# Products of two heads given to TensorE in turn, on different rows or columns of its array

## The chip, the core and the metric

The kernel runs on one core of a Trainium2 chip, as one launch. The metric is the device time of that launch in microseconds (us): the median of three runs of the kernel before is 3310.76 us (3308.05 to 3312.59). The profiled execution is a run of its own; its trace lists each instruction with its engine, its line in the kernel and the names of the tiles it writes and reads. PE is TensorE, DVE VectorE, ACT ScalarE, POOL GpSimd.

## The reference

Two layers act on 512 latent tokens and 256 context tokens of width 1024. Each layer is: half-step SwiGLU feed-forward, token mixing, half-step SwiGLU feed-forward, each with RMS norm and a shift, scale and gate from a conditioning vector. Token mixing projects the tokens with one matrix and gives the columns to four groups of heads that work side by side. Their outputs are concatenated and projected back.

- GLA: 4 heads with keys of 32 and values of 64, gated linear attention in chunks of 64 tokens, both directions in time.
- Mamba-2 (SSD): 4 heads of 64 in 2 groups with a state of 64, chunks of 64, both directions.
- RWKV-7: 4 heads of 64, a recurrence whose state is changed by a rank-one term at each token, both directions.
- Attention: 4 query heads and 2 key heads of 64, softmax over latents and context.

The second layer needs no context output. The products in question are the small ones inside the chunks, for instance in GLA

```
q_dec = q * jnp.exp(b)
att = jnp.einsum('bnthd,bnshd->bnhts', q_dec, k * jnp.exp(-b))
att = jnp.where(causal, att, 0.0)
```

and in SSD `cb = einsum('bctgn,bcsgn->bcgts', cc, bc)`. For RWKV-7 the kernel does not step token by token: it writes a chunk as products of 64x64 matrices, with the inverse of a triangular matrix for the rank-one terms.

## The kernel before, in words

Activations lie transposed, features on the 128 partitions and tokens along the free dimension. So a head of 64 features occupies 64 partitions and two heads (a pair, index `hp`, and `e` or `hh` within it) fill one tile. A product of one head has its contraction on 64 (GLA: 32) of the array's 128 rows, or its output on 64 of the 128 columns. All of these products are float32, and the program's float32 product appears in the trace as two MATMUL records (called passes here), each with its own weight load.

`mix` (L1783 on) runs one layer's token mixing in two stages. The first stage opens pools with two PSUM banks for the tag `pg` (GLA), two for `ps` (SSD and RWKV preparation) and two double banks for the projections (`proj`, tile `pj`). In program order it holds:

- `rwkv_inverses`, which calls `x_rwkv_n` for each direction, pair and block of 256 tokens: per head four 64x64 products, a masking on DVE (L1330) and two DMAs to a DRAM tile `nd`. From `nd`, `x_rwkv_inverse` (L1398 on) later inverts the triangular matrices on DVE, 31 steps of two instructions (L1410, L1412) per direction.
- `x_gla_in`, `x_gla_dir`, `x_ssm_in`, then `x_gla_block` (L931) per block: per head four products into one bank `pg`, a masking on DVE (L944) into `am`, an addition on POOL into `a2`.
- `x_ssm`: per block and group two products (tile `cb`, L1077 to L1086), each group masked on DVE.
- The two inversions, the gates, the attention's inputs and the last projections.

The second stage (`open_second`, then `rwkv`) has three PSUM banks `pr` for RWKV, two `pc` for its recurrent steps, two `sc` and one `po`. The order of RWKV's pieces is written out by hand in `SCHEDULE`: U prepares a unit (one direction, one block; `x_rwkv_unit`), S solves it (`x_rwkv_solve`), T makes one recurrent step per chunk of 64 (`x_rwkv_step`), Y forms the outputs of a block (`x_rwkv_y`). There are six units per layer. The output projection of the other groups (`x_out`, tiles `yp`, `woh`, `wol`) and the attention (`x_att`) are written behind it.

The program's order is only the input of the framework's planner: the planner simulates the engines with its own costs and lays a fixed order for each engine. Each engine then takes its instructions in that order; PE's queue has products of projections, `x_out` and attention laid between RWKV's.

The places that the change touches:

- `x_rwkv_n`: head after head; both heads write partitions 64 to 127 of a bank of their own, and each is masked alone with 64 partitions.
- `x_rwkv_unit`: per pair, head `e` after head `e` (contraction on rows `es`), each in its own bank `pr`, each followed by one or two maskings (L1377). Then transposes (L1381), then eight products per pair into partitions 64 to 127 of one bank per pair, copied by ACT to the lower half of `ZV`; then transposes of `Bh` (L1394).
- `x_rwkv_solve`: after the solve, the product `pw` runs with its two heads in turn on different columns (`pw[64 * e:64 * e + 64, ...]`); the last eight products per pair go to partitions 64 to 127 of one bank per pair, copied back to `ZV`.
- `x_rwkv_y`: for every chunk and pair one product of 128 rows and columns with the state `H`, then two products of 128 rows and 64 columns (`ZV` with `A1`).

Of the kernel before, what the change touches and what calls it, by code (L numbers as in the profile page):

```python
# [7 lines left out]
F32 = mybir.dt.float32  # L8
# [4 lines left out]
ALU = mybir.AluOpType  # L13
# [5 lines left out]
D = 1024  # L19
# [33 lines left out]
class Net:  # L53
# [877 lines left out]
    def x_gla_block(self, l, b, D, yg):  # L931
        nc, gw = self.nc, self.gw
        mask = self.c("mgb", 256).rearrange("p (d t) -> p d t", d=2).unsqueeze(1).to_broadcast([128, 2, 2, 128])
        am = []
        for hh in range(4):
            hs = slice(32 * hh, 32 * hh + 32)
            pa = self.bank("pg")
            for tt in range(2):
                t = 2 * b + tt
                ts = slice(128 * t, 128 * t + 128)  # L940
                for d in range(2):
                    self.mm(pa[:, 256 * tt + 128 * d:256 * tt + 128 * d + 128], D[d][1][hs, ts], D[d][0][hs, ts])
            w = gw.tile([128, 2, 2, 128], F32, tag="am", name="am")
            nc.vector.tensor_tensor(w, pa.rearrange("p (t d x) -> p t d x", t=2, d=2), mask, op=ALU.mult)  # L944
            a2 = gw.tile([128, 2, 128], F32, tag=f"a2{hh}", name="a2", bufs=1)
            nc.gpsimd.tensor_tensor(a2, w[:, :, 0], w[:, :, 1], op=ALU.add)
            am.append(a2)
# [115 lines left out]
    def x_ssm(self, l, F, dts, need_ctx):  # L1063
        nc, gw = self.nc, self.gw
        nt = NT if need_ctx else NX
        blocks = (2, 0, 1) if need_ctx else (0, 1)
        x0, x1, Bf, Cf = F
# [7 lines left out]
        cb = [self.gt(f"cb{g}", (6, 128)) for g in range(2)]  # L1075
        both = self.c("bones", 128)
        for b in blocks:  # L1077
            for g in range(2):
                gs = slice(64 * g, 64 * g + 64)
                pb = self.bank("ps")  # L1080
                for tt in range(2):
                    t = 2 * b + tt
                    ts = slice(128 * t, 128 * t + 128)
                    self.mm(pb[:, 128 * tt:128 * tt + 128], Bf[gs, ts], Cf[gs, ts])
# [6 lines left out]
        for g in range(2):  # L1091
# [48 lines left out]
        for d in range(2):  # L1140
# [20 lines left out]
            for r in range(2):  # L1161
# [3 lines left out]
                pss = [self.bank("ps"), self.bank("ps")]  # L1165
                for n in order:
                    t, e = divmod(n, 2)
                    es = slice(64 * e, 64 * e + 64)
                    for g in range(2):
                        self.mm(pss[e][64 * g:64 * g + 64, 64 * t:64 * t + 64], BT[es, t, 64 * g:64 * g + 64], xw[r][es, t, g])  # L1170
                for n, nx in zip(order, order[1:]):
                    t, e = divmod(n, 2)
                    nc.vector.scalar_tensor_tensor(out=Sr[:, nx], in0=Sr[:, n], scalar=dec[r][:, n:n + 1],
                                                   in1=pss[e][:, 64 * t:64 * t + 64], op0=ALU.mult, op1=ALU.add)
            for b in blocks:
                bs = slice(256 * b, 256 * b + 256)
# [136 lines left out]
    def x_rwkv_n(self, hp, d, b, U, dec, nd):  # L1313

        nc, gw = self.nc, self.gw
        kk, bb = U
        P, iP = dec
        cs = slice(4 * b, 4 * b + 4)
        w = lambda z: z[:, 256 * b:256 * b + 256].rearrange("p (c t) -> p c t", t=64)
        mask = self.c("mr", 256)[64:128, 128 * d:128 * d + 64].unsqueeze(1).to_broadcast([64, 4, 64])  # L1320
# [3 lines left out]
        A = self.gx.tile([128, 2, 4, 64], F32, bufs=2, tag="wb", name="ns")  # L1324
        for hh in range(2):
            hs = slice(64 * hh, 64 * hh + 64)
            pss = self.bank()
            for c in range(4):
                self.mm(pss[64:128, 64 * c:64 * c + 64], R[hs, c, 0], R[hs, c, 1])
            nc.vector.tensor_tensor(A[64:128, hh], pss[64:128, 0:256].rearrange("p (c t) -> p c t", c=4), mask, op=ALU.mult)  # L1330
            for i in range(2):
                self.load(nd[i, hp, hh, cs].rearrange("c s t -> s c t"),
                          A[64 + 32 * i:96 + 32 * i, hh, :, 32 * i:32 * i + 32])

    def x_rwkv_unit(self, l, d, b, U, PC, ld, want):


        nc, rw = self.nc, self.rw
        r, k, v, kk, bb = U
        P, iP = self.x_rwkv_decay_of(b, ld)  # L1340
        mask = self.c("mr", 256)[:, 128 * d:128 * d + 128].rearrange("p (a t) -> p a t", a=2)
        cs = slice(4 * b, 4 * b + 4)
        w = lambda z: z[:, :, 256 * b:256 * b + 256].rearrange("p h (c t) -> p h c t", t=64)
        self.nR += 1
        tag = ("gqk", "R", "vT")[self.nR % 3]
        R = rw(tag, (2, 4, 3, 64)) if tag == "R" else self.room(tag, (2, 4, 3, 64))
# [3 lines left out]
        B = rw("B", (2, 4, 2, 64))  # L1350
# [15 lines left out]
        nc.gpsimd.memset(ZU[0:64], 0.0)  # L1366
        na = 2 if want else 1
        for hp in range(2):
            for e in range(2):
                ps = self.bank()  # L1370
                es = slice(64 * e, 64 * e + 64)
                for c in range(4):
                    self.mm(ps[:, 128 * c:128 * c + 64 * na], B[es, hp, c].rearrange("p a t -> p (a t)"),
                            R[es, hp, c, 1:1 + na].rearrange("p a t -> p (a t)"))
                pv = ps.rearrange("p (c a t) -> p c a t", c=4, a=2)
                for i, o in ((0, A0[:, hp, e]), (1, A1[:, hp, :, e, 0]))[:na]:
                    nc.vector.tensor_tensor(o, pv[:, :, i], mask[:, i].unsqueeze(1).to_broadcast([128, 4, 64]), op=ALU.mult)  # L1377
        for hp in range(2):
# [5 lines left out]
        for hp in range(2):  # L1384
            pa = self.bank()
            for c in range(4):
                for e in range(2):
                    u = 64 * (2 * c + e)
                    self.mm(pa[64:128, u:u + 64], A0[:, hp, e, c], ZV[:, hp, c, e])
            self.copy(flat(ZV)[64:128, 512 * hp:512 * hp + 512], pa[64:128])  # L1390
        for hp in range(2):
            pt = self.bank()
            for c in range(4):
# [23 lines left out]
    def x_rwkv_solve(self, d, b, unit, td, pd):  # L1417
        nc, rw = self.nc, self.rw
        A0, A1, ZV, ZU, R = unit
# [23 lines left out]
                    self.mm(pw[64 * e:64 * e + 64, u:u + 64], ZU[:, hp, c, e], A0[:, hp, e, c])  # L1443
        WT = rw(f"WT{self.nR % self.UNITS[1]}", (2, 4, 64))
        nc.vector.tensor_copy(WT.rearrange("p h c t -> p (h c t)"), pw)
        for hp in range(2):
            pu = self.bank()
            for c in range(4):
                for e in range(2):
                    u = 64 * (2 * c + e)  # L1450
                    self.mm(pu[64:128, u:u + 64], A0[64:128, hp, e, c], ZV[64:128, hp, c, e])
            self.copy(ZV.rearrange("p h c e t -> p (h c e t)")[64:128, 512 * hp:512 * hp + 512], pu[64:128])
        return WT

    def x_rwkv_step(self, d, n, unit, WT, PC, H, Hn):

# [24 lines left out]
    def x_rwkv_y(self, b, unit, Hs, ya, add):  # L1481

        A0, A1, ZV, ZU, R = unit
        py = self.bank().rearrange("p (h c t) -> p h c t", h=2, c=4)
        for c, H in enumerate(Hs):
            for hp in range(2):
                if H is not None:
                    self.mm(py[:, hp, c], H[:, hp].rearrange("p e x -> p (e x)"), R[:, hp, c, 2], True, False, skip=True)
                for e in range(2):
                    self.mm(py[64 * e:64 * e + 64, hp, c], ZV[:, hp, c, e], A1[:, hp, c, e, 0], H is None, True, skip=True)  # L1490
# [529 lines left out]
```

## Time and profile before

| | |
|---|---|
| median of three runs | 3310.76 us |
| profiled execution, its own time | 3308.48 us |
| its span, first to last instruction | 3306.7 us |
| mean granted TensorE clock over the span | 0.954 |
| PE busy | 3119.4 us, 94% of the span, 21012 instructions |
| DVE busy | 2486.1 us, 75%, 4697 instructions |
| ACT busy | 1256.2 us, 38% |
| POOL busy | 930.5 us, 28% |

Busy time of PE is a union of modelled durations: a float32 pass of 64 columns appears as some 230 ns long although the next one starts 58 ns later, so a busy PE may still wait for a short while. The distance from the start of one group to the start of the next is the better measure, and the timeline shows it. The two mixing stages lie at about 590 to 1250 us and 2360 to 2900 us of the span; the rest is feed-forward and norms.

### The profile page before, as it was taken

To read this page: it belongs to the slowest core of one execution; us is meant where nothing else is said; L and a number is where in the kernel's file an instruction comes from. 1 tells how busy PE (TensorE), PEld (TensorE's weight loads), DVE (VectorE), ACT (ScalarE), POOL (GpSimd) and SP (SyncE) were. 2 spreads that over 40 slices of the span, in tenths; PEclk is the share of its full clock that TensorE was granted. 3 is DMA by queue.
4 is the path that set the end of the run, shared out by engine and by line. 5 is a ranking of instruction groups with operands and counts; after the bars stand their busy time and mean duration, and the time that the engine had idled before them with its cause. 6 is when DMAs were issued, how large, how long until landed. Compare 5 with 4: busy or idle time off the path is not lost.

```text
span 3306.7 us, 54832 instructions
## 1 busy us (share of the span) xinstructions
PE 3119.4 (94%) x21012; PEld 2756.4 (83%) x21012; DVE 2486.1 (75%) x4697; ACT 1256.2 (38%) x2256; POOL 930.5 (28%) x776
## 2 busy tenths in 40 slices
PE   6999999999889988999999999999899789989999
PEld 4899999777778767899998899999777668679998
DVE  7999898567955347888888787777657855387878
ACT  3333334342233434333334333333443244344444
POOL 0133333234232100233331132324145332003433
PEclk9999999999889989999999999999999879989999
DMA  6344444223232022233443233332324231033233
GB/s 250 100 130 142 138 133 134 66 76 100 68 108 76 9 74 86 90 122 127 125 131 96 71 115 109 115 115 93 112 64 113 78 105 37 5 119 115 90 102 122
DMA packets 184342, 335.74 MB, mean 102 GB/s; under 512 B 64753, under 2 KB 80977, under 8 KB 183697
## 3 DMA queue, kind: packets, MB, share of 16 engines
q1 hardware_dynamic: 184080, 332.25, 31.8%
q8 instruction: 165, 2.70, 0.3%
q14 instruction: 97, 0.79, 0.1%
HBM read 304.99 MB, written 27.18 MB: 100 GB/s over the span
## 4 chain that ended last, share of the span: by engine, by line
PE 43%; DVE 6%; DMA 1%; issue 1%; ACT 1%; POOL 0%; SPq 0%; DVEq 0%; ACTq 0%; POOLq 0%
PE pt L63 32%; PE pj L63 3%; PE pr L63 3%; PE sc L63 1%; DVE wlo L78 1%; PE ps L63 1%; PE po L63 1%; PE pc L63 1%; DVE inv L1412 1%; DVE T L1410 1%; PE pg L63 0%; DVE t L345 0%; DVE hl L348 0%; DMA sg<-cd 0%; DVE X L358 0%
## 5 line engine op out<-in xcount | busy, mean ns | idle before, releaser
L77 ACT ACTIVATE whi<-wraw 128x512 fp32r<-128x512 f32 (+1 forms) x624 | 379.1, 617 | 705.0 <-PE pt L63 413.0
L63 PE MATMUL pt<-g,whi 128*128 128x512 f32 (+1 forms) x2528 | 631.9, 342 | 11.2 <-DVE X L358 5.8
L63 PE MATMUL pt<-hh,whi 128*128 128x384 f32 (+2 forms) x1664 | 532.2, 326 | 26.7 <-ACT hh L347 14.6
L63 PE MATMUL pt<-hl,whi 128*128 128x384 f32 (+2 forms) x1664 | 539.2, 325 | 5.4 <-DVE hl L348 5.1
L63 PE MATMUL pt<-hh,wlo 128*128 128x384 f32 (+2 forms) x1664 | 534.9, 324 | 0.1
L63 PEld LDWEIGHTS pt<-g,whi 128*128 128x128 f32 x2528 | 436.0, 190 | 69.9 <-DVE g L78 4.1
L78 DVE TENSOR_TENSOR wlo<-wraw,whi 128x512 fp32r<-128x512 f32 (+1 forms) x536 | 436.5, 824 | 37.2 <-ACT whi L77 35.6
L63 PE MATMUL pt<-g,wlo 128*128 128x512 f32 (+1 forms) x1264 | 422.6, 340 | 0.0
L63 PE MATMUL pt<-T,whi 128*128 128x384 f32 (+1 forms) x1728 | 406.4, 322 | 0.4 <-DVE s L544 0.4
L522 POOL TENSOR_TENSOR ws<-wraw 128x512 f32<-128x512 f32 x72 | 117.4, 1631 | 1015.5 <-DMA wraw<-in_ffn_in 723.9
L206 DVE SCALAR_TENSOR_TENSOR junk<-wm,cb 128x1024 bf16<-128x1024 f32 x272 | 358.7, 1319 | 1.9 <-DMA wm<-in_w_mod 1.7
L63 PEld LDWEIGHTS pt<-hh,whi 128*128 128x128 f32 x1664 | 317.1, 192 | 38.4 <-ACT hh L347 19.0
L63 PEld LDWEIGHTS pt<-hl,whi 128*128 128x128 f32 x1664 | 318.3, 191 | 16.8 <-DVE hl L348 7.8
L63 PEld LDWEIGHTS pt<-hh,wlo 128*128 128x128 f32 x1664 | 316.9, 191 | 8.4 <-DVE wlo L78 0.5
L358 DVE SCALAR_TENSOR_TENSOR X<-pt,hg,X 128x512 f32<-128x512 f32 (+1 forms) x376 | 224.4, 614 | 119.0 <-PE pt L63 116.3
L63 PEld LDWEIGHTS pt<-T,whi 128*128 128x128 f32 x1728 | 299.6, 188 | 1.5 <-DVE s L544 0.9
L77 ACT ACTIVATE whi<-ws 128x512 fp32r<-128x512 f32 x288 | 180.6, 629 | 291.0 <-PE pt L63 213.5
L78 DVE TENSOR_TENSOR wlo<-ws,whi 128x512 fp32r<-128x512 f32 x288 | 259.1, 902 | 26.6 <-ACT whi L77 25.6
L63 PE MATMUL pt<-T,wlo 128*128 128x384 f32 (+1 forms) x864 | 276.2, 322 | 0.0
L63 PEld LDWEIGHTS pt<-g,wlo 128*128 128x128 f32 x1264 | 239.1, 189 | 26.9 <-DVE wlo L78 0.2
L78 POOL TENSOR_TENSOR wlo<-wraw,whi 128x512 fp32r<-128x512 f32 x88 | 127.3, 1450 | 318.7 <-ACT whi L77 298.9
L63 PE MATMUL pj<-hh,whi 128*128 128x512 f32 x616 | 190.3, 374 | 10.7 <-DVE k L1226 5.8
(450 smaller groups left out, 5469.6 us busy)
## 6 DMA issues: line engine op xcount, KB each, us to landing
wraw<-in_ffn_in SPq DMA_DIRECT2D x176, 512.0 KB, 3.6
wm<-in_w_mod SPq DMA_DIRECT2D x144, 512.0 KB, 3.7
wraw<-in_ffn_out SPq DMA_DIRECT2D x192, 256.0 KB, 2.7
wraw<-in_w_in SPq DMA_DIRECT2D x88, 256.0 KB, 2.8
wraw<-in_w_out SPq DMA_DIRECT2D x32, 256.0 KB, 3.2
xd<-X SPq DMA_DIRECT2D x16, 384.0 KB, 2.6
wraw<-in_ffn_out SPq DMA_DIRECT2D x32, 128.0 KB, 2.0
wa<-in_w_out SPq DMA_DIRECT2D x16, 256.0 KB, 3.0
```

The costliest lines, as they stand in the source:

```text
L63: self.nc.tensor.matmul(out, lhsT=lhsT, rhs=rhs, start=start, stop=stop, skip_group_check=skip)
L77: self.nc.scalar.activation(out=hi, in_=src, func=AF.Copy)
L78: (eng or self.nc.vector).tensor_tensor(lo, src, hi.bitcast(F32), op=ALU.subtract)
L206: nc.vector.scalar_tensor_tensor(out=junk, in0=w, scalar=1.0, in1=self.cb[:, s], op0=ALU.mult, op1=ALU.mult, accum_out=self.mod[l][:, s, j ...
L358: self.nc.vector.scalar_tensor_tensor(out=self.X[j][:, sg], in0=o, scalar=self.hg[l][:, s, 8 * n + j:8 * n + j + 1], in1=self.X[j][:, sg], ...
L522: nc.gpsimd.tensor_tensor(w1, a21, a22, op=ALU.add)
L1410: nc.vector.tensor_tensor(tv, N[:, s, tt].unsqueeze(2).to_broadcast([96, nt, nj]), X[:, s, jj].unsqueeze(1).to_broadcast([96, nt, nj]), op ...
L1412: nc.vector.tensor_tensor(X[:, tt, jj], X[:, tt, jj], tv, op=ALU.add)
```

## The change

- `x_gla_block`: two heads at a time. Their products alternate, one on each head's 32 rows, into two banks `pg` taken together; then each is masked and added as before.
- `x_ssm` (`cb`): the same with the two groups, on 64 rows each, in two banks `ps`.
- `x_rwkv_n`: the two heads alternate; each writes its own 64 partitions of one bank, and a single masking of 128 partitions replaces two of 64. The stores' number and size stay.
- `x_rwkv_unit`: the two heads of a pair alternate, in two banks `pr` taken together; the maskings follow.
- `heads_apart` (new) replaces the two loops at the end of the unit and of the solve: head 0 writes partitions 0 to 63 and head 1 partitions 64 to 127 of one bank for both pairs, the two alternate, and two ACT copies (one per head instead of one per pair) follow all 16 products.
- `x_rwkv_y`: all products with `H` first, then all those of `ZV` with `A1`. Only the first product of the bank has the start flag.

The diff, cut to its core:

```
 x_gla_block
+        for h0 in (0, 2):
+            pas = [self.bank("pg") for _ in range(2)]
             for tt in range(2):
...
                 for d in range(2):
+                    for i in range(2):
+                        hs = slice(32 * (h0 + i), 32 * (h0 + i) + 32)
+                        self.mm(pas[i][:, ...], D[d][1][hs, ts], D[d][0][hs, ts])
+            for i, pa in enumerate(pas):
...
 x_ssm
+            pbs = [self.bank("ps") for _ in range(2)]
+            for tt in range(2):
...
+                for g in range(2):
+                    gs = slice(64 * g, 64 * g + 64)
+                    self.mm(pbs[g][:, 128 * tt:128 * tt + 128], Bf[gs, ts], Cf[gs, ts])
+            for g, pb in enumerate(pbs):
...
 x_rwkv_n
+        mask = self.c("mr", 256)[:, 128 * d:128 * d + 64].unsqueeze(1).to_broadcast([128, 4, 64])
...
+        A = self.gx.tile([128, 4, 64], F32, bufs=2, tag="wb", name="ns")
+        pss = self.bank()
+        for c in range(4):
+            for hs in (slice(0, 64), slice(64, 128)):
+                self.mm(pss[hs, 64 * c:64 * c + 64], R[hs, c, 0], R[hs, c, 1])
+        nc.vector.tensor_tensor(A, pss[:, 0:256].rearrange(...), mask, op=ALU.mult)
...
 x_rwkv_unit
         for hp in range(2):
+            pss = [self.bank() for _ in range(2)]
+            for c in range(4):
+                for e in range(2):
+                    es = slice(64 * e, 64 * e + 64)
+                    self.mm(pss[e][...], B[es, hp, c]..., R[es, hp, c, 1:1 + na]...)
+            for e, ps in enumerate(pss):
...
+        self.heads_apart(self.bank(), lambda hp, c, e: (A0[:, hp, e, c], ZV[:, hp, c, e]), ZV)
 x_rwkv_solve
+        self.heads_apart(self.bank(), lambda hp, c, e: (A0[64:128, hp, e, c], ZV[64:128, hp, c, e]), ZV)
+        return WT
+
+    def heads_apart(self, ps, of, ZV):
+        halves = (slice(0, 64), slice(64, 128))
         for hp in range(2):
             for c in range(4):
+                for e, es in enumerate(halves):
+                    u = 64 * (4 * hp + c)
+                    self.mm(ps[es, u:u + 64], *of(hp, c, e))
+        for e, es in enumerate(halves):
+            self.copy(ZV[64:128, :, :, e], ps[es].rearrange("p (h c t) -> p h c t", h=2, c=4))
 x_rwkv_y
+        first = True
         for c, H in enumerate(Hs):
+            for hp in range(2 if H is not None else 0):
+                self.mm(py[:, hp, c], H[:, hp]..., R[:, hp, c, 2], first, False, skip=True)
+                first = False
+        for c in range(4):
             for hp in range(2):
                 for e in range(2):
+                    self.mm(py[64 * e:64 * e + 64, hp, c], ZV[:, hp, c, e], A1[:, hp, c, e, 0], False, True, skip=True)
```

## Rows read from the trace of the kernel before

**Rows 1.** The page's 40 slices: busy tenths of PE, and the granted clock.
```profile
PE   6999999999889988999999999999899789989999
PEclk9999999999889989999999999999999879989999
```

**Rows 2.** Windows: length, busy PE, PEld, DVE, ACT, POOL (count), PEclk, DMA, GB/s.
```profile
690.00:770.00 80.00, 79.12 (x677) 63.45 (x676) 67.33 (x116) 35.97 (x52) 32.70 (x29) 0.91 0.32 85
850.00:960.00 110.00, 85.38 (x707) 74.27 (x707) 82.24 (x245) 33.99 (x44) 38.36 (x41) 0.84 0.25 73
960.00:1150.00 190.00, 188.98 (x1952) 155.29 (x1950) 84.94 (x185) 73.97 (x124) 46.50 (x62) 0.92 0.22 62
2610.00:2690.00 80.00, 56.50 (x419) 46.38 (x418) 61.88 (x182) 27.23 (x43) 30.84 (x36) 0.70 0.25 73
2690.00:2850.00 160.00, 158.23 (x1725) 126.28 (x1723) 72.62 (x163) 66.72 (x111) 40.21 (x57) 0.96 0.20 54
```

**Rows 3.** Chain of work that ended last, second mixing stage: start, length, what.
```profile
2537.76 1.08 PE pg L63 x8
...
2628.68 1.22 DVE T L1410
...
2689.44 2.36 PE pr L63 x32
```

**Rows 4.** PE's timeline around `pw` and the loops after it: start, length, passes.
```profile
988.30 1.15 PE L63 MATMUL pr<-A,ZU 128*64 128x64 f32 x32
989.38 2.08 PE L63 MATMUL pr<-ZV,A 64*64 64x64 f32 x32
...
1002.92 2.08 PE L63 MATMUL pr<-ZV,A 128*64 128x64 f32 x32
```

**Rows 5.** PE's timeline through one unit.
```profile
1119.08 1.16 PE L63 MATMUL pr<-gqk,B 64*128 64x128 f32 x8
...
1121.18 1.71 PE L63 MATMUL pr<-gqk,B 64*128 64x128 f32 x16
```

**Rows 6.** PE's timeline in one output block, and eight passes of 128 columns.
```profile
1040.35 0.43 PE L63 MATMUL pr<-R,H 128*128 128x64 f32 x2
1040.72 0.34 PE L63 MATMUL pr<-A,ZV 128*64 128x64 f32 x4
1040.98 0.43 PE L63 MATMUL pr<-R,H 128*128 128x64 f32 x2
...
1060.88 1.09 PE L1381 MATMUL pr<-cst,R 128*128 128x128 f32 x8
```

**Rows 7.** PE's timeline in the first stage: RWKV's, GLA's and SSD's products.
```profile
730.47 0.67 PE L63 MATMUL ps<-nr 64*64 64x64 f32 x8
...
787.42 1.20 PE L63 MATMUL pg<-qd,gS 32*64 32x64 f32 x32
...
790.26 0.71 PE L63 MATMUL ps<-F,F 64*128 64x128 f32 x4
790.90 1.15 PE L63 MATMUL pg<-qd,kn 32*128 32x128 f32 x8
```

**Rows 8.** Groups by line and form: PE, DVE (590 to 1000), ACT (960 to 1150).
```profile
L63 PE MATMUL ps<-nr 64*64 64x64 f32 x384 | 29.0, 230 | 2.0 <-DVE ns L1330 1.9
L63 PE MATMUL pg<-qd,kn 32*128 32x128 f32 x160 | 21.0, 290 | 2.1 <-DVE gqk L964 2.1
L1330 DVE TENSOR_TENSOR ns<-ps,cst 64x256 f32<-64x256 f32 x24 | 9.8, 427 | 3.2 <-PE ps L63 2.7
L944 DVE TENSOR_TENSOR am<-pg,cst 128x512 f32<-128x512 f32 x12 | 7.9, 682 | 2.4 <-PE pg L63 2.4
L1377 DVE TENSOR_TENSOR A<-pr,cst 128x256 f32<-128x256 f32 x16 | 5.7, 416 | 2.5 <-PE pr L63 2.5
L815 ACT ACTIVATE ZV<-pr 64x512 f32<-64x512 f32 x35 | 20.7, 592 | 38.4 <-PE pr L63 20.3 <-PE pr L1381 17.4 <-POOL Hd L1466 0.4
```

More of the change, by code (lines that the diff above doesn't have):

```diff
@@ L934, in x_gla_block @@
         am = []
-        for hh in range(4):
-            hs = slice(32 * hh, 32 * hh + 32)
-            pa = self.bank("pg")
+        for h0 in (0, 2):
+            pas = [self.bank("pg") for _ in range(2)]
             for tt in range(2):
@@ L941, in x_gla_block @@
                 for d in range(2):
[L942 to L947, printed above, removed]
+                    for i in range(2):
+                        hs = slice(32 * (h0 + i), 32 * (h0 + i) + 32)
+                        self.mm(pas[i][:, 256 * tt + 128 * d:256 * tt + 128 * d + 128], D[d][1][hs, ts], D[d][0][hs, ts])
+            for i, pa in enumerate(pas):
+                w = gw.tile([128, 2, 2, 128], F32, tag="am", name="am")
+                nc.vector.tensor_tensor(w, pa.rearrange("p (t d x) -> p t d x", t=2, d=2), mask, op=ALU.mult)
+                a2 = gw.tile([128, 2, 128], F32, tag=f"a2{h0 + i}", name="a2", bufs=1)
+                nc.gpsimd.tensor_tensor(a2, w[:, :, 0], w[:, :, 1], op=ALU.add)
+                am.append(a2)
         for hp in range(2):
@@ L1077, in x_ssm @@
         for b in blocks:
[L1078 to L1084, printed above, removed]
+            pbs = [self.bank("ps") for _ in range(2)]
+            for tt in range(2):
+                t = 2 * b + tt
+                ts = slice(128 * t, 128 * t + 128)
+                for g in range(2):
+                    gs = slice(64 * g, 64 * g + 64)
+                    self.mm(pbs[g][:, 128 * tt:128 * tt + 128], Bf[gs, ts], Cf[gs, ts])
+            for g, pb in enumerate(pbs):
                 nc.vector.tensor_tensor(cb[g][:, 2 * b:2 * b + 2], pb[:, :256].rearrange("p (t x) -> p t x", t=2),
@@ L1319, in x_rwkv_n @@
         w = lambda z: z[:, 256 * b:256 * b + 256].rearrange("p (c t) -> p c t", t=64)
-        mask = self.c("mr", 256)[64:128, 128 * d:128 * d + 64].unsqueeze(1).to_broadcast([64, 4, 64])
+        mask = self.c("mr", 256)[:, 128 * d:128 * d + 64].unsqueeze(1).to_broadcast([128, 4, 64])
         R = gw.tile([128, 4, 2, 64], F32, tag="am", name="nr")
@@ L1323, in x_rwkv_n @@
         self.decayed(d, w(kk), w(P), R[:, :, 1])
-        A = self.gx.tile([128, 2, 4, 64], F32, bufs=2, tag="wb", name="ns")
-        for hh in range(2):
[L1326 to L1330, printed above, removed]
+        A = self.gx.tile([128, 4, 64], F32, bufs=2, tag="wb", name="ns")
[3 more added lines that the diff above has]
+                self.mm(pss[hs, 64 * c:64 * c + 64], R[hs, c, 0], R[hs, c, 1])
+        nc.vector.tensor_tensor(A, pss[:, 0:256].rearrange("p (c t) -> p c t", c=4), mask, op=ALU.mult)
+        for hh in range(2):
             for i in range(2):
                 self.load(nd[i, hp, hh, cs].rearrange("c s t -> s c t"),
-                          A[64 + 32 * i:96 + 32 * i, hh, :, 32 * i:32 * i + 32])
+                          A[64 * hh + 32 * i:64 * hh + 32 * i + 32, :, 32 * i:32 * i + 32])
     def x_rwkv_unit(self, l, d, b, U, PC, ld, want):
@@ L1368, in x_rwkv_unit @@
         for hp in range(2):
[L1369 to L1373, printed above, removed]
+            pss = [self.bank() for _ in range(2)]
+            for c in range(4):
+                for e in range(2):
+                    es = slice(64 * e, 64 * e + 64)
+                    self.mm(pss[e][:, 128 * c:128 * c + 64 * na], B[es, hp, c].rearrange("p a t -> p (a t)"),
                             R[es, hp, c, 1:1 + na].rearrange("p a t -> p (a t)"))
+            for e, ps in enumerate(pss):
                 pv = ps.rearrange("p (c a t) -> p c a t", c=4, a=2)
@@ L1383, in x_rwkv_unit @@
             self.copy(flat(ZU)[64:128, 512 * hp:512 * hp + 512], pt[64:128])
[L1384 to L1390, printed above, removed]
+        self.heads_apart(self.bank(), lambda hp, c, e: (A0[:, hp, e, c], ZV[:, hp, c, e]), ZV)
         for hp in range(2):
@@ L1445, in x_rwkv_solve @@
         nc.vector.tensor_copy(WT.rearrange("p h c t -> p (h c t)"), pw)
+        self.heads_apart(self.bank(), lambda hp, c, e: (A0[64:128, hp, e, c], ZV[64:128, hp, c, e]), ZV)
+        return WT
+    def heads_apart(self, ps, of, ZV):
+        halves = (slice(0, 64), slice(64, 128))
         for hp in range(2):
-            pu = self.bank()
             for c in range(4):
[L1449 to L1453, printed above, removed]
+                for e, es in enumerate(halves):
[3 more added lines that the diff above has]
+            self.copy(ZV[64:128, :, :, e], ps[es].rearrange("p (h c t) -> p h c t", h=2, c=4))
     def x_rwkv_step(self, d, n, unit, WT, PC, H, Hn):
@@ L1484, in x_rwkv_y @@
         py = self.bank().rearrange("p (h c t) -> p h c t", h=2, c=4)
+        first = True
         for c, H in enumerate(Hs):
+            for hp in range(2 if H is not None else 0):
+                self.mm(py[:, hp, c], H[:, hp].rearrange("p e x -> p (e x)"), R[:, hp, c, 2], first, False, skip=True)
+                first = False
+        for c in range(4):
             for hp in range(2):
-                if H is not None:
-                    self.mm(py[:, hp, c], H[:, hp].rearrange("p e x -> p (e x)"), R[:, hp, c, 2], True, False, skip=True)
                 for e in range(2):
-                    self.mm(py[64 * e:64 * e + 64, hp, c], ZV[:, hp, c, e], A1[:, hp, c, e, 0], H is None, True, skip=True)
+                    self.mm(py[64 * e:64 * e + 64, hp, c], ZV[:, hp, c, e], A1[:, hp, c, e, 0], False, True, skip=True)
         yb = ya[:, :, 256 * b:256 * b + 256].rearrange("p h (c t) -> p h c t", c=4)
```

## The prediction

> **What bounds the kernel now.** I read the page's slices first, then windows of the mixing stages, the chain of waits, and PE's timeline group by group. In the slices the reader is to see that PE is at nine tenths nearly everywhere and that its clock leaves the upper level only in the mixing stages [rows 1]. All edits lie there, so the feed-forward's time stays.
>
> Mixing is not one stage. In RWKV's stage PE is busy 188.98 of 190 us in the first layer and 158.23 of 160 in the second, with DVE, ACT and POOL below half [rows 2]. There PE's work is the time. In 690 to 770, where `x_rwkv_n` runs, PE is at 79.12 of 80 but DVE also at 67.33. In 850 to 960 PE is busy 85.38 of 110 and DVE 82.24, and in 2610 to 2690 PE only 56.50 of 80: there the inversions on DVE set the pace [rows 2]. The chain agrees: GLA's products of PE at 2538, a step of the inversion on DVE at 2629, and from 2689 PE with tile `pr` [rows 3]. So a microsecond of PE taken from RWKV's stage is mostly a microsecond of the kernel; one taken before the inversions is so only in part.
>
> **What one pass costs.** The timeline has the same work in both forms. `pw` is 32 passes of 128 rows and 64 columns whose two heads alternate between the column halves: length 1.15 us. The two loops that become `heads_apart` are 32 passes of the same 64 columns, all on the upper column half: 2.08 us each, with the contraction on 64 rows as with 128 [rows 4]. So alternating halves the time on columns, and what counts is the number of columns, not of rows.
>
> For rows the evidence is less direct. In GLA's block 32 passes of 64 columns, two heads on different rows and columns and into one bank, last 1.20 us [rows 7], against 2.08 on one place [rows 4]. A unit's eight passes of one head last 1.16 us, but sixteen of two heads back to back 1.71 rather than twice that [rows 5]: the second head starts while the first is still running. I take it that a pair of heads in turn costs what one head costs now. The bounds are that (rows fully apart) and no gain at all.
>
> Lengths hold a tail of 0.07 to 0.08 us that the next group covers; I take it off below.
>
> **The change part by part**, at the upper clock level:
>
> *`heads_apart`.* Two loops per unit, 12 units in two layers, 24 loops. Each falls from 2.08 to 1.15 as `pw` shows: 0.93 x 24 = 22.3 us of PE. The two ACT copies of 592 ns [rows 8] stay two, but both now wait for all 16 products, where the first pair's copy could start halfway. Queued behind them on ACT are the next copies and the exponentials of attention; ACT is busy 73.97 of 190 [rows 2], which covers it. PE waits for the copies only before the recurrent steps; uncovered that is about 0.6 us per loop, 14 in all.
>
> *`x_rwkv_unit`.* Per unit now 8 + 16 + 8 passes: 1.16 + 1.71 + 1.16 less three tails = 3.8 us. After: two pairs of 1.08 = 2.2. That is 1.6 x 12 = 19.6 us. The change adds a wait: a pair takes two of the three banks `pr` at once, so the second pair's head 1 needs the first pair's head 0 to be masked, two maskings of 416 ns [rows 8]. Behind that product PE's queue holds the transposes and whatever the planner laid there. Uncovered it costs at most 0.9 us per unit, 11 in all, and leaves 9; covered by attention or `x_out` products it costs nothing.
>
> *`x_rwkv_y`.* Now a cycle of two `H` passes and four `ZV` passes takes 0.63 us (1040.98 less 1040.35 [rows 6]), and there are eight: 5.0 us. The two `H` passes alone take 0.37 of it, since each change between the full array and its halves is paid for. After: 16 passes of 128 columns at 0.13 (eight last 1.09 [rows 6]) = 2.0, and 32 alternating passes as `pw`, 1.08: 3.1. That is 1.9 x 10 blocks (six and four) = 19.2 us. Nothing is added; the `H` of all four chunks exist by then because the schedule puts Y behind the fourth step or later.
>
> These three sum to 61 us in RWKV's two stages. Of that I take three quarters, 46: the stage has other engines at about 45% and 40% [rows 2], and the recurrent steps, loads and copies that PE covers now will sometimes be late. The bounds are none of it and all.
>
> *`x_rwkv_n`.* 48 groups of 8 passes (384 [rows 8]) of 0.60 us [rows 7] become 24: 14 us of PE at most. 48 maskings of 427 ns (24 in the first layer [rows 8]) become 24 on twice the partitions; one of 128 partitions and the same 256 elements takes 416 [rows 8], so DVE saves 24 x 0.43 = 10 us. The store of each head still waits for its masking, and now for the other head too: at most 0.6 us later, with the inversions a hundred us behind.
>
> *`x_gla_block`.* 160 passes, 21.0 us busy [rows 8], in 20 groups of 8 of 1.08 [rows 7]; ten groups after: 10 us. Both `pg` banks are taken at once, so the next pair waits for two maskings of 682 ns [rows 8]; PE has projections and SSD products to lay between. Uncovered it is 1.4 us, ten times, more than the gain: from -10 to +4.
>
> *`x_ssm`.* Ten groups of 4 passes of 0.64 [rows 7] become five: 3 us.
>
> These make 27 us of PE and 10 of DVE in stretches where both are full or the inversions decide. I count 10 us, nearer to the low end, because the chain passes through the inversions afterwards [rows 3]. The bounds are -4 and 27.
>
> Here a rule of the Trainium skill speaks against one edit. The page TensorEngine Tiling (Array Packing), Restrictions and Gotchas, "Gotcha 1: PSUM Pressure", says that different row tiles cannot access the same PSUM bank at the same time; `x_rwkv_n` now writes one bank from two row tiles, on different partitions. By the rule its 14 us would not come, and the sum would be some 5 us smaller. The 1.20 us above are two row tiles writing different partitions of one bank at once, so this case's trace does not bear it out, and I keep the gain.
>
> **Sum.** 46 + 10 = 56 us off the profiled execution's 3308.5 gives 3252.5. The median of the runs stands 2.3 us above that execution, so I predict 3254.
>
> **Rivals.**
>
> *A. What follows PE sets the pace.* After the products are paired, maskings and copies do not get faster. A unit's eight maskings take 8 x 0.416 = 3.3 us on DVE, against 3.8 for its products now: 0.5 x 12 = 6 us instead of 19.6. A `heads_apart` loop has two copies of 0.592, 1.18 us against 2.0: 0.82 x 24 = 20. The outputs keep 19. Three quarters of 45 is 33, nothing from the first stage: 3277. For it: three banks. Against: DVE waits in RWKV's stage at 84.94 of 190 [rows 2], and PE has other products to lay between. The Trainium skill's page on TensorEngine Tiling states this as a rule under "PSUM Bottleneck": tiling speeds up TensorE but not the evacuation of PSUM.
>
> *B. All of it arrives, and clock with it.* 61 + 27 from above. RWKV's windows have granted clocks of 0.92 and 0.96 [rows 2], that is 30 and 13 us at the lower level (twice the missing share, times 190 and 160), which cost half, 21 us; if the denser products spare half of that, 10 more: 3308.5 - 98 + 2 = 3212. For it: PE at 99%. Against: the inversions.
>
> *C. Different rows do not run at once.* Then only columns and outputs gain: 22.3 + 19.2, three quarters, 31 us: 3279. Against it: sixteen passes in 1.71 us [rows 5].
>
> *D. Slower, by the clock.* PE ends its small products sooner and waits; the clock falls. Place: RWKV's two windows, 350 us, 304 after the gain. In 2610 to 2690, where PE waits for the inversions, the clock is 0.70 [rows 2]. At that clock 182 of 304 us are at the lower level (43 now), 139 more, which costs 70 us: 3252.5 + 70 + 2 = 3325. It decides from 112 more us at the lower level, a mean clock of about 0.75 there, where the 56 us are used up. For it: waits are added in front of PE in two places. Against: the planner has attention and `x_out` to fill with, and two heads at once keep more of the array at work.
>
> **How the numbers follow.** The forecast has 0.52, with a range of its own from 3236 to 3272; A 0.20, B 0.13, C 0.06, D 0.09. The range for 8 in 10 runs from 3212 (B) to 3292 (A and C, with some more lost to a worse order by the planner), leaving out D and the edge of B. This measurement can tell about 0.2%, 7 us, from no change. All cases but D lie further than that on the faster side; with a little for A falling short: faster 0.89, within 0.2% 0.03, slower 0.08.
>
> **What would show it.** After the change the 32 passes of either loop of `heads_apart` should last about 1.15 us as `pw` does; a pair of heads in a unit 1.2 for 16 passes; an output block 3.1 instead of 5.0; a pair in `x_rwkv_n` 0.67 for 16. If 16 passes of a unit still last 1.7 to 2.2, C holds. If they are short but RWKV's stages shrink by less than half of 61 us, with PE waiting for DVE L1377's successor or the `ZV` copies, A holds. RWKV's stages should shrink by some 23 us each, and the stretch before them by about 5. A granted clock below 0.8 in those stages would make the forecast wrong on D's side; a longer inversion stretch would be the planner's doing.

## The result, and the profile after

Four runs of the changed kernel took 3270.17, 3283.64, 3266.95 and, disturbed and left out of the ratio, 7426.26 us. The ratio to the kernel before is 0.9884 with an interval from 0.9854 to 0.9914: 1.16% faster, about 38 us (28 to 48). The profiled execution took 3270.17 us, span 3268.4, against 3308.48 and 3306.7.

The slices of the changed kernel first: busy tenths of PE, then the granted clock in tenths ([rows 1]). PE's look like those of before; the clock reads 8 or less in eleven slices in and around the mixing stages, where before it was six.

```profile
PE   6999999899989988999999999999899879989999
...
PEclk9999999998889988999999999999898879889999
```

The five windows of [rows 2], in the changed kernel: length, busy PE, PEld, DVE, ACT, POOL (count), granted clock, DMA share, GB/s.

```profile
690.00:770.00 80.00, 72.47 (x665) 57.16 (x664) 66.06 (x120) 35.48 (x54) 32.65 (x27) 0.91 0.35 89
850.00:960.00 110.00, 90.98 (x678) 79.88 (x668) 72.46 (x219) 37.28 (x49) 38.91 (x37) 0.89 0.26 83
960.00:1150.00 190.00, 184.57 (x2115) 147.66 (x2116) 104.34 (x232) 81.87 (x140) 52.71 (x77) 0.97 0.22 62
2610.00:2690.00 80.00, 63.25 (x430) 52.20 (x431) 50.29 (x114) 30.57 (x51) 33.04 (x38) 0.72 0.34 99
2690.00:2850.00 160.00, 155.35 (x1701) 118.52 (x1698) 81.27 (x199) 68.81 (x115) 35.35 (x56) 0.94 0.13 32
```

RWKV's windows hold more of DVE and ACT than before in the same time, which fits a stage that runs faster (the table below has its length). Its chain ([rows 3]) is as it was: GLA's products on PE, a step of the inversion on DVE, and from 2646 PE with tile `pr`.

```profile
2535.68 1.44 PE pg L63 x8
...
2611.09 1.41 DVE inv L1412
...
2646.52 3.67 PE pr L63 x24
```

I cut both executions at the same marks: a stage of RWKV runs from the first product of a unit to the last of an output block, a tail from there to the last product of the output projection (`pt` with `y`).

| stretch | before | after | difference | at the lower clock, before and after |
|---|---|---|---|---|
| RWKV's two stages | 435.2 | 393.9 | -41.3 | 77 and 69 us |
| first stages (first `x_rwkv_n` to first unit) | 497.6 | 495.5 | -2.1 | 125 and 155 |
| tails of mixing | 130.7 | 127.4 | -3.3 | 36 and 25 |
| the rest (feed-forward, and mixing up to the first `x_rwkv_n`) | 2243.2 | 2251.5 | +8.3 | 65 and 77 |

The last column is worked out from the granted clock, which in the records is either full or half (2.4 or 1.2 GHz): twice the share missing from full speed, times the length. Where PE sets the pace, half of that time is what the lower level cost. Taken off, RWKV's stage went from 212 to 192 us in the first layer and from 185 to 167 in the second, 20 and 18 less. As they ran, 33 and 9 came: the time at the lower clock fell by 26 us in the first and rose by 18 in the second.

**The loops that pay.** PE's timeline of the changed kernel, rows that answer to [rows 4] and [rows 6]: start, length, passes.

```profile
991.52 1.15 PE L63 MATMUL pr<-A,ZU 128*64 128x64 f32 x32
992.61 1.15 PE L63 MATMUL pr<-ZV,A 64*64 64x64 f32 x32
...
1004.39 0.69 PE L63 MATMUL pr<-ZV,A 128*64 128x64 f32 x16
...
1036.47 1.55 PE L63 MATMUL pr<-R,H 128*128 128x64 f32 x12
1037.95 1.15 PE L63 MATMUL pr<-A,ZV 128*64 128x64 f32 x32
```

The loop of `heads_apart` that took 2.08 us takes 1.15, as `pw` above it, and the output's products by form stand in two clean groups. Summed from start to start of consecutive products, the two loops went from 51.5 to 29.4 us, the outputs from 50.0 to 31.6.

**The loops that don't.** The same view, a unit ([rows 5]) and GLA's and `x_rwkv_n`'s products ([rows 7]).

```profile
700.67 0.68 PE L63 MATMUL ps<-nr 64*64 64x64 f32 x16
...
711.25 1.12 PE L63 MATMUL ps<-nr 64*64 64x64 f32 x16
...
786.37 1.71 PE L63 MATMUL pg<-qd,kn 32*128 32x128 f32 x16 [1.12 <-DVE gqk L967]
...
789.42 2.07 PE L63 MATMUL pg<-qd,kn 32*128 32x128 f32 x8
795.25 2.07 PE L63 MATMUL pg<-qd,kn 32*128 32x128 f32 x8 [3.75 <-DVE am L947]
...
1045.87 1.16 PE L63 MATMUL pr<-R,B 64*128 64x128 f32 x8
1047.38 1.16 PE L63 MATMUL pr<-R,B 64*128 64x128 f32 x8
1049.49 1.71 PE L63 MATMUL pr<-R,B 64*128 64x128 f32 x16
```

A unit is as before: 8, 8 and 16 passes of 1.16, 1.16 and 1.71. The order built for PE's queue says why. It is the planner's, and of a pair written in turn it made this (bank, products):

```
pr_9614 x4    pr_9615 x4        (a unit's pair: head 0, then head 1)
pg_7301 x4    pg_7302 x4        (a pair in GLA)
```

Of 24 pairs in the units 4 kept their turns, 6 did in part, 14 stand head after head; of 10 pairs in GLA one kept them, another nearly. These are the edits in which each head has a bank of its own. Where both heads share one bank (`heads_apart`, `x_rwkv_n`) the turns are kept. That the second bank is the planner's reason is not shown: no run gave such a pair a single bank. GLA's eight passes now often take 2.07 us: the clock is at its lower level from 788.6 on, for 44 us. Just before, PE had waited 1.12 us for `gqk`, and inside that time 3.75 us for a masking. The groups ([rows 8]) of the changed kernel, by line and form:

```profile
L63 PE MATMUL pg<-qd,kn 32*128 32x128 f32 x160 | 25.7, 334 | 5.8 <-DVE am L947 4.1 <-DVE gqk L967 1.1 <-DVE gS L922 0.6
L63 PE MATMUL ps<-nr 64*64 64x64 f32 x384 | 17.4, 241 | 1.8 <-DVE PC L1296 1.3 <-DVE nr L1315 0.4
...
L947 DVE TENSOR_TENSOR am<-pg,cst 128x512 f32<-128x512 f32 x12 | 8.1, 684 | 8.6 <-PE pg L63 8.6
L1334 DVE TENSOR_TENSOR ns<-ps,cst 128x256 f32<-128x256 f32 x12 | 4.9, 411 | 3.7 <-DMA nd<-ns 3.6
```

12 maskings of 411 ns stand where 24 of 427 stood.

### The profile page after: what moved, and what is told of

It is laid out like the page before. It is cut to its first block, busy times and chain, and to the rows that moved or that the text cites. A ratio compares the mean times of both kernels' runs of the same rounds, so it can differ in the third digit from the quotient of the medians.

```text
span 3268.4 us, 54830 instructions
## 1 busy us (share of the span) xinstructions
PE 3073.0 (94%) x21012; PEld 2718.5 (83%) x21012; DVE 2470.5 (76%) x4673; ACT 1254.7 (38%) x2256; POOL 931.5 (28%) x776
## 4 chain that ended last, share of the span: by engine, by line
PE 76%; DVE 14%; DMA 4%; issue 2%; ACT 2%; SPq 1%; POOL 0%; DVEq 0%; ACTq 0%; POOLq 0%
PE pt L63 55%; PE pj L63 6%; PE pr L63 4%; PE sc L63 3%; DVE wlo L78 2%; PE pg L63 2%; PE ps L63 2%; PE po L63 1%; DVE inv L1412 1%; DVE T L1410 1%; PE pc L63 1%; SPq L60 1%; DVE t L345 1%; DMA sg<-cd 1%; DVE X L358 1%
## 5 line engine op out<-in xcount | busy, mean ns | idle before, releaser
L78 DVE TENSOR_TENSOR wlo<-ws,whi 128x512 fp32r<-128x512 f32 x288 | 258.3, 899 | 26.2 <-ACT whi L77 25.2
L63 PEld LDWEIGHTS pt<-g,wlo 128*128 128x128 f32 x1264 | 239.2, 189 | 26.6
```

The lines of the kernel that those rows point to most:

```text
L63: self.nc.tensor.matmul(out, lhsT=lhsT, rhs=rhs, start=start, stop=stop, skip_group_check=skip)
L78: (eng or self.nc.vector).tensor_tensor(lo, src, hi.bitcast(F32), op=ALU.subtract)
```

## The experiments

All runs are listed here first. PE's sums and the time at the lower clock are from the one profiled execution of each; "rest" is its span less half of the time at the lower clock, an estimate of what it would be at full clock if PE alone set the pace. "unit", "nr" and "GLA" are the products of `x_rwkv_unit`'s first loop, `x_rwkv_n` and `x_gla_block`, from start to start, waits behind them included. The kernel with only an order exchanged (`n3_hp_unit`) has a rest 7 us off before's, so I don't read differences below that.

| run | ratio to before, interval | unit | nr | GLA | lower clock | rest | rest, mean of runs |
|---|---|---|---|---|---|---|---|
| before | 1 | 47.8 | 26.6 | 20.1 | 304 | 3155 | 3155 |
| e1_heads_apart | 0.9983, 0.9969 to 0.9996 | 55.9 | 26.0 | 21.8 | 330 | 3141 | 3140 |
| e2_outputs | 0.9898, 0.9883 to 0.9913 | 49.7 | 25.7 | 22.7 | 253 | 3150 | 3142 |
| e3_pairs | 0.9946, 0.9926 to 0.9966 | 50.6 | 26.0 | 18.9 | 264 | 3152 | 3144 |
| e4_one_mask | 1.0079, 1.0057 to 1.0101 | 53.0 | 19.1 | 33.4 | 410 | 3144 | 3141 |
| n3_hp_unit | 1.0004, 0.9990 to 1.0017 | 48.5 | 25.7 | 19.9 | 307 | 3148 | 3150 |
| changed kernel | 0.9884, 0.9854 to 0.9914 | 50.0 | 18.6 | 29.2 | 326 | 3105 | 3104 |
| e5_no_pairs | 0.9901, 0.9883 to 0.9919 | 48.7 | 19.9 | 35.1 | 294 | 3129 | 3121 |
| e6_forced_unit | 0.9820, 0.9803 to 0.9838 | 37.7 | 16.7 | 32.7 | 266 | 3114 | 3106 |
| e7_forced_all | 0.9752, 0.9732 to 0.9773 | 37.9 | 19.2 | 15.9 | 267 | 3094 | 3098 |
| e8_old_n | 0.9811, 0.9790 to 0.9832 | 45.5 | 25.9 | 18.3 | 230 | 3121 | 3120 |
| e11_unit_old_n | 0.9834, 0.9820 to 0.9847 | 38.7 | 26.2 | 19.0 | 264 | 3122 | 3117 |
| e13_all_old_n | 0.9762, 0.9746 to 0.9777 | 39.9 | 25.7 | 16.1 | 233 | 3100 | 3105 |
| e14_two_masks | 0.9872, 0.9857 to 0.9888 | 50.3 | 20.1 | 25.1 | 307 | 3118 | 3119 |

One execution is a thin base: the rest of a single run lies up to 9 us from the mean of its kernel. But every run has its granted clock on record, and its span times that clock is its rest; the last column is the mean over the runs that the ratio rests on. By it the four parts alone take 15, 13, 11 and 14 us off, 53 together, and the whole change 51. At full clock the parts nearly add up, and of the 51 us the lower clock took 13 back.

### Each part of the change alone, on the kernel before

What I expected of each run stands under its edit; "theory T" is defined in the first.

`e1_heads_apart`:

```diff
 x_rwkv_unit, x_rwkv_solve
-        for hp in range(2):
-            pa = self.bank()
...
+        self.heads_apart(self.bank(), lambda hp, c, e: (...), ZV)
```

> The kernel before with the two heads_apart loops alone. In the changed kernel the two loops took 22 us less of PE (51.5 to 29.4, sums of intervals between starts). Theory T (the edits that keep a pair in one bank alternate on PE and pay; the edits that need two banks were laid out as before by the planner and pay nothing): 15 to 22 us faster, loops at 1.08 to 1.15 us for 32 passes. Rival A (what follows PE sets the pace): under 12 us, PE waiting for the ZV copies before pw and the steps.

`e2_outputs` takes only the new `x_rwkv_y`:

```diff
+        for c, H in enumerate(Hs):
+            for hp in range(2 if H is not None else 0):
...
+        for c in range(4):
+            for hp in range(2):
+                for e in range(2):
```

> The kernel before with x_rwkv_y by form alone. The changed kernel has 18 us less of PE in these products. Theory T: 12 to 18 us faster, an output block 3.1 us of PE where it was 5.0. Rival A: also about that, since nothing follows faster; a smaller gain (under 9 us) would say that the stage does not pass PE time on to the end.

`e3_pairs` takes only the pairs that need two banks:

```diff
 x_rwkv_unit (and, with pg and ps, x_gla_block and x_ssm)
+            pss = [self.bank() for _ in range(2)]
+            for c in range(4):
+                for e in range(2):
```

> The kernel before with the three two-bank edits alone: x_rwkv_unit's pairs, x_gla_block, x_ssm. My prediction gave them 19.6, 10 and 3 us of PE. Theory T: no gain, 0 to 15 us slower; most 16-pass groups of a unit still at 1.7 us, PE's order with the four products of one bank ahead of the four of the other; GLA's products with more time at the lower clock. Rival A: pairs alternate (16 passes in 1.2 us) and 6 us are gained, the rest waiting for maskings. The forecast's own view: 15 to 25 us faster.

`e4_one_mask` takes only the new `x_rwkv_n`:

```diff
+        pss = self.bank()
+        for c in range(4):
+            for hs in (slice(0, 64), slice(64, 128)):
...
+        nc.vector.tensor_tensor(A, pss[:, 0:256]..., mask, op=ALU.mult)
```

> The kernel before with x_rwkv_n alone (two heads in one bank, one masking). The changed kernel's products of it took 8 us less of PE, my forecast 14. Theory T: 3 to 10 us faster; pairs of 16 passes near 0.7 us where they stand back to back. Rival A, or a stage whose end is set by DVE and the inversions: within 3 us of before.

Measured, by the ratios: -6, -34, -18 and +26 us (the medians, which later expectations quote, give -6, -33, -21 and +28). None fell where theory T had it. e1 lies in rival A's range and e3 in that of the forecast's own view, but not for the reasons given: in e1's RWKV stages PE waited for a copy of `ZV` once, 1.9 us, and in e3 the pairs' products took about as long as before. The sum of the four (-0.9%) is near the whole change (-1.2%) all the same. PE's own sums did as T said: in e1 the loops went from 51.5 to 30.4 us, in e2 the outputs from 50.0 to 29.2, in e3 the unit's products gained nothing, in e4 `nr` fell by 7.5.

What differs is the time at the lower clock. Take PE's saving in the edited products at full clock (half of their own time at the lower clock left out) and add half of the change of that time in the profiled execution: e1 -20 + 13 = -7, e2 -18 - 25 = -43, e3 about -2 - 20 = -22, e4 -9 + 53 = +44. Signs and order come out, sizes within 20 us (the profiled execution of e4 was 42 us slower than before's; its median run less). In e1 the second RWKV stage lost at the lower clock what the loops had won (199 us before, 207 in e1); here are the same unit's passes in e1 and, in the second fence, in the kernel before, at the lower and at the full clock:

```profile
2698.36 1.96 PE L63 MATMUL pr<-vT,B 64*128 64x64 f32 x8
2701.83 1.97 PE L63 MATMUL pr<-vT,B 64*128 64x64 f32 x8
```

```profile
2710.11 1.10 PE L63 MATMUL pr<-vT,B 64*128 64x64 f32 x8
```

In e4 `x_rwkv_n` is done at 732 instead of 763, but GLA's products do not start much earlier (770 for 777), and from 793 its stretch runs at the lower level for 41 us. PE waited there 5.3 us for the masking of `am`; after that it is busy without a pause.

```profile
796.61 2.07 PE L63 MATMUL pg<-qd,kn 32*128 32x128 f32 x8 [5.32 <-DVE am L944]
```

The window 800 to 850 of e4 (columns as above):

```profile
800.00:850.00 50.00, 50.00 (x454) 41.53 (x451) 33.25 (x93) 5.92 (x11) 8.85 (x11) 0.66 0.20 68
```

From this I formed theory O: an edit's own PE time arrives, but the planner's new order also moves time between the clock's two levels.

### Taking parts out of the changed kernel, holding the turns, and a null edit

`e8_old_n` undoes `x_rwkv_n`, `e5_no_pairs` undoes the three pairs with two banks; their diffs are those of e4 and e3 with the signs exchanged.

> The changed kernel with x_rwkv_n as before. Alone the masking edit cost 28 us (3339 against 3311), and its profile has 411 us at the lower clock where before has 305, 41 of them in one piece in GLA's stretch of the first layer (788 to 830 in the changed kernel too). Theory O (an edit's own PE time arrives, but the planner's new order also moves the time at the lower clock, by up to 50 us of gain or loss): 3235 to 3263, if the four single effects add up 3250; clock of 770 to 850 back above 0.82. Theory T (only two-bank edits fail): one masking gains, so 3280 to 3290 without it.

> The changed kernel with x_rwkv_unit's pairs, x_gla_block and x_ssm as before. Alone these edits gained 21 us although their products took no less of PE (unit 47.8 to 50.6, GLA 20.1 to 18.9), and 38 us less at the lower clock. Theory T (they bring nothing): 3262 to 3282, as the changed kernel. If their 21 us are a property of the edits: 3290 to 3305. Theory O: the difference to the changed kernel is half the difference of the time at the lower clock, of either sign.

`e6_forced_unit` is e5 with a unit's pairs held in turn. `issue_after` fixes a place in the queue's order and adds no wait:

```diff
+            self.turned = None
             for c in range(4):
-                for e in range(2):
+                for e in (1, 0):
...
-                    self.mm(pss[e][...], ...)
+                    self.in_turn(pss[e][...], ...)
+    def in_turn(self, *a):
+        if self.turned:
+            with self.tc.issue_after(self.turned):
+                self.mm(*a)
+        else:
+            self.mm(*a)
+        self.turned = self.told(mybir.EngineType.PE)
```

> The changed kernel with GLA and SSD as before and a unit's pairs held in alternation on PE (each product given behind the one of the other head). Against the run without pairs: theory T expects 16 passes in 1.2 us where they took 1.7, unit's products 15 to 20 us less of PE and 8 to 18 us less time. Rival A (the second bank is not free and PE waits for maskings of 0.42 us): passes short, but PE idle ahead of each pair, gain under 4 us or a loss.

`n3_hp_unit`:

```diff
 x_rwkv_unit, the first loop, kernel before
-        for hp in range(2):
+        for hp in (1, 0):
```

> The kernel before with the two pairs of heads of x_rwkv_unit's first loop given in the opposite order (pair 1, then pair 0): the same instructions on the same data, but another order from the planner. Theory O: the time moves by more than 7 us either way, up to 25, by half the change of the time at the lower clock. Theory T: within 7 us of before.

e8: 3250 us, near the sum of the single effects, as O had it. e5: within the interval of the changed kernel, as T had it; the pairs bring nothing there, though they brought 18 us alone, and O's half of the change at the lower clock (e5 16 us faster) did not show. The null edit moved nothing (T right, O wrong): it has 307 us at the lower clock, before 304, so not every new order moves the clock.

e6 is 0.8% faster than e5, 27 us where T had 8 to 18. PE's timeline of e6, two pairs of a unit:

```profile
1042.81 0.48 PE L63 MATMUL pr<-R,B 64*128 64x128 f32 x2
1043.89 1.16 PE L63 MATMUL pr<-R,B 64*128 64x128 f32 x14
...
1071.18 1.16 PE L63 MATMUL pr<-vT,B 64*128 64x128 f32 x16
```

Sixteen passes of two heads in turn last 1.16 us, exactly what eight of one head last in the changed kernel. So the pairs do run at once, and it was the order that kept them apart. A unit's products fell by 11.0 us, not 20: in most pairs the planner lays the first product (two passes) apart, and these last 0.48 by themselves.

### Both steps together, and one masking taken apart

`e11_unit_old_n` is the changed kernel with e6's `in_turn` in the unit and `x_rwkv_n` as before. `e13_all_old_n` adds the same `in_turn` in GLA and SSD:

```diff
 x_gla_block (and x_ssm, with pbs)
-                    for i in range(2):
+                    for i in (1, 0):
...
-                        self.mm(pas[i][...], ...)
+                        self.in_turn(pas[i][...], ...)
```

> The changed kernel with x_rwkv_n as before and a unit's pairs held in alternation. The two steps alone gave 27 us (3277 to 3250, x_rwkv_n as before) and 29 us (3278 to 3248, alternation held, against the run without pairs). Theory O (two separate causes: the planner undoes the unit's alternation, 10 us of PE; and one masking empties GLA's stretch of projections, so that it runs at the lower clock): they add up, 3220 to 3238, unit's products near 36 us. Rival: both gains are the same time at the lower clock, won once: 3242 to 3252.

> The same with the pairs of x_gla_block and x_ssm held in alternation too. My prediction gave them 13 us of PE. Theory O: their products take 6 to 10 us less of PE, and since the first stage waits for maskings and inversions and its length follows the clock, between 5 us faster and 10 us slower than the run without holding them. Rival (that stage passes PE time on): 6 to 12 us faster.

`e14_two_masks`, on the changed kernel:

```diff
 x_rwkv_n
-        nc.vector.tensor_tensor(A, pss[:, 0:256]..., mask, op=ALU.mult)
         for hh in range(2):
+            hs = slice(64 * hh, 64 * hh + 64)
+            nc.vector.tensor_tensor(A[hs], pss[hs, 0:256]..., mask[hs], op=ALU.mult)
```

> The changed kernel with x_rwkv_n's two heads in one bank and in turn as now, but masked one after the other on 64 partitions each. This keeps the edit's saving of PE and gives DVE its work back. If the shorter masking is what packs x_rwkv_n's groups and leaves GLA's stretch at the lower clock (theory O): GLA's stretch of the first layer back at a clock above 0.82, 3240 to 3262. If it is the shared bank or the alternation: 3268 to 3285, GLA's stretch below 0.75.

`e7_forced_all` is e13 with `x_rwkv_n` as changed.

> The changed kernel with all three kinds of pairs held in alternation, x_rwkv_n as changed (one bank, one masking). Against the same with x_rwkv_n as before (3229) it shows that edit on a third base; it cost 28 us alone and 27 in the changed kernel. If the cost belongs to the edit: 3249 to 3260, GLA's stretch of the first layer (800 to 850) at a clock under 0.85. If it belonged to the order that the other pairs happened to have: 3215 to 3238.

e11: 3256, slower than either theory had it; against e8 the unit's products fell by 6.8 us and nothing came of it (intervals overlap). So e6's 27 us against e5 are not the turns' alone: 11 are PE's in these products, and 14 are half of the 27 us less at the lower clock; in e11 the profile has 34 us more of it than in e8.

e13: 3229, 0.7% faster than e11, and more than either expected; e7 is 0.7% faster than e6 likewise. Holding GLA's and SSD's turns is worth 22 to 24 us on both bases (against heads in sequence in e6, against turns written but not held in e11). In e13 GLA's products account for 3 us of it (19.0 to 16.1), in e7 for 17, so why the gains are alike is not shown. In e7, PE's timeline of GLA, and the window 800 to 850:

```profile
771.97 1.15 PE L63 MATMUL pg<-qd,kn 32*128 32x128 f32 x14
...
792.13 0.79 PE L63 MATMUL pg<-qd,kn 32*128 32x128 f32 x2 [4.59 <-DVE gqk L968]
...
798.37 1.15 PE L63 MATMUL pg<-qd,kn 32*128 32x128 f32 x14
```

```profile
800.00:850.00 50.00, 49.99 (x638) 42.13 (x634) 38.96 (x104) 9.98 (x17) 18.16 (x20) 1.00 0.24 80
```

The same 50 us hold 638 matmul records instead of e4's 454, at the full clock instead of 0.66. GLA's products fell from 32.7 us in e6 to 15.9, and the first stages from 495 to 468.

e14: 3268, at the near edge of the second reading, with the clock of its stretch, 0.81, just short of the first; `x_rwkv_n` ends as early (731) as with one masking. It settles nothing beyond that the number of maskings isn't what packs these products.

e7: 3225, level with e13. On this third base one masking costs nothing, where it had cost 26 us alone and 24 in the changed kernel (0.9884 against 0.9811). So the cost was not the edit's own. In all three comparisons the mean rest is smaller with it (by 14, 16 and 7 us); what it cost was at the lower clock. Which of the held turns took the cost away is not separated: already e6, with one masking, a unit's turns held and GLA's heads in sequence, is no slower than e11 with two (0.9820 against 0.9834). e7 and e13 are the fastest kernels here, 2.4% below before.

**What stays open.** Which feature of an order sends a stretch to the lower clock. The runs show where it happens and what it costs. With one masking and GLA's turns not held (e4, e5, e6, the changed kernel) PE waits there in one piece 3.8 to 5.8 us for the masking of `am`, and 27 to 44 us in one piece are at the lower clock. In e7, with the turns held, neither is there; but PE waits 4.6 us for `gqk` and only 7 us in one piece are at the lower clock, so a wait alone doesn't decide it. The runs do not show why e2 spends 51 us less there and e1 26 more.

## Why the prediction was right, and where it wasn't

The direction and the range held (3212 to 3292); of the 56 us that I forecast off the profiled execution 38 came.

- *`heads_apart`*: 22.3 us of PE forecast, 22.1 measured (some 20 of it at full clock; the rest is less time at the lower). The pattern of `pw` held to the digit (1.15).
- *`x_rwkv_y`*: 19.2 forecast, 18.4 measured.
- *`x_rwkv_unit`*: 19.6 forecast, none came (47.8 to 50.0; at full clock some 3, with ten of 24 pairs at least partly in turn). This is the step that failed. "I take it that a pair of heads in turn costs what one head costs now" is true of the engine: 1.16 us for 16 passes when held in turn. What I did not price is that the planner may lay a pair in another order than the program. I charged the second bank as a wait for maskings; instead the planner put most pairs head after head, and in RWKV's stages PE showed no wait for these maskings.
- *Three quarters of the sum*: RWKV's stages lost 41.3 us, near the 46 forecast, but by errors that cancel, which is luck. At full clock they lost 37 of the 41 us that `heads_apart`, the outputs and the unit saved there, so a tenth was due and not a quarter; the unit's 19.6 were nearly all missing; and 8 us less at the lower clock gave 4 more. I had named 23 us for each stage: 33 and 9 came, by the clock.
- *First stages*: 10 us forecast, 2 came. `x_rwkv_n` gave 8 of 14 us: its groups had taken 26.6 us before, not 48 times 0.60, and the packed ones ran partly at the lower level (0.68 and 1.12 us for the same 16 passes). SSD gave nothing. GLA's products took 9 us more instead of 10 less: mostly head after head as before, with 7 us for the lower clock and 4 for waits behind them. In all, 29 us more of these stages were spent at the lower clock; without half of it, 15 us, they would be some 16 us shorter than before (an estimate, since PE does not set the pace all through them).
- *The rest*: 0 forecast, 5 us longer outside these stages; 12 us more of it at the lower clock. I had read from the slices that the clock leaves its upper level only in mixing. A 9 there hides up to a tenth: 41 us of the feed-forward were at the lower level already before.

Of the rivals, C's sign appeared (16 passes of a unit still at 1.71) without C: e6 shows that different rows do run at once. The sign I had named could not tell "does not overlap" from "is not in turn". A's sign appeared in GLA (3.75 us for `am`), hardly in RWKV's stage. D's mechanism was at work, but in the first stage and for 15 us, not in RWKV's for 70.

I had weighed a rule of the Trainium skill (page TensorEngine Tiling (Array Packing), Restrictions and Gotchas, "Gotcha 1: PSUM Pressure": different row tiles cannot use one PSUM bank at the same time). The trace of the changed kernel doesn't bear it out for different partitions of a bank: `x_rwkv_n`'s 16 passes into one bank take 0.68 us, as long as 8 did [rows 7]. The "PSUM Bottleneck" section of the same page of the Trainium skill warns of the evacuation. In e6, with a unit's turns held, PE waited from 940 to 1150 only 0.8 us for maskings of `A` and 2.1 for copies of it, and from 2620 to 2825 1.4 and, copies of `ZV` included, 4.6; so here it did not become the bound.

## What to carry to other kernels

Where a planner lays the final order, read that order before pricing an interleaving: here it took apart most pairs with a buffer for each head and none of those that share one, and an explicit order on the queue put the turns back (e7 is another 1.3% faster). Read a measured gain in two parts, PE's time at full clock and half of the change of the time at the lower clock. Here the first could be priced ahead, the second not. Measure single edits on more than one base: the same edit was worth +26, +24 and 0 us, another -27 and +8.

## What the runs showed of the hardware that I had not expected

Sixteen passes of 128 columns from two heads on different rows took 1.16 us with 64 rows each (e6) and fourteen with 32 rows each 1.15 (e7), the time of eight from one head (1.16 and 1.15): the second head costs nothing more. Given head after head, as in the changed kernel's 16 passes of 1.71 us, the second head's first pass starts 0.55 us after the first head's (1050.041 and 1049.486 in its trace), together with the fifth of that head's eight: a part of the overlap comes without turns, too. And in the trace PE can be busy without a pause, 50.00 of 50 us, with the clock granted at 0.66 (e4), while 49.99 of 50 busy with more work in it had 1.00 (e7).
